# Gated delta rule: the small parts of each head at sixteenths of a head's time, and 11 loads ahead of the overflow loop instead of 14

## The chip, the cores and the metric

The kernel runs on one core of a Trainium2 chip, in one launch. TensorE (PE) multiplies matrices, VectorE (DVE), ScalarE (ACT) and GpSimd (POOL) work on what it leaves in PSUM and on SBUF, and SyncE (SP) issues most of the DMAs. The metric is the device time of the program in microseconds (us), as the median of several runs.

## The reference

A sequence of 512 tokens of width 1024 passes through two blocks. The first has a mixer (a gated delta rule with 8 heads, an HGRN2 recurrence with 8 heads, two gated branches that are merged), cross attention over 256 memory tokens, and a mixture of 32 experts of which each token takes two; the second is two layers of a hybrid of retention, sparse attention and RG-LRU. The change touches the delta rule and the experts.

The delta rule, of one head with chunks of the sequence (q, k, v come from projections, a causal convolution of width 4 and SiLU; q and k are normalised):

```
decay = exp(cum_i - cum_j) for i >= j
A     = strictly lower part of (beta k) k^T * decay
u, w  = (I + A)^-1 [beta v, beta k exp(cum)]
for each chunk:
    v_new = u - w S
    o     = (q exp(cum)) S + (q k^T * decay) v_new
    S     = S exp(last) + (k exp(last - cum))^T v_new
y = rmsnorm(o) * silu(gate)
```

The experts: each token goes to its two best experts of its best group, and `y = (silu(x Wgate) * (x Wup)) Wdown`, weighted and summed over the two. An expert takes 64 tokens at its fixed place; tokens beyond these go through a loop with a run-time number of turns, the overflow loop.

## The kernel before, in words

**The mixer's delta rule (lines 612 to 850, called from `mixer`).** Each head needs four blocks of 128 columns of the projections: q, k, v and the gate g. A block (`Blocks.steps`, lines 275 to 288) is 8 steps over the contraction of 1024; a step is three matmuls of 128 x 128 by 512 columns (`mm3`, lines 218 to 220), since both operands are held as a rounded and a remaining part. In its third step a block also emits the next block's load and its split into two parts (`w_hi` on ACT, line 154, `w_lo` on DVE, line 155).

Beside the blocks run the head's small parts, each a generator that emits a few instructions and yields: `keys` (convolution and SiLU of k, its norm, k k^T, and the way of the matrix A through DRAM into another layout), `queries`, `values`, `gate_out`, `substitute` (36 small operations on DVE, line 743, that invert the 16 x 16 diagonal blocks, then DRAM again), `inverse` (seven steps that build the inverse of I + A from these blocks by matmuls of 64 x 64, the last at line 810, copied by DVE into `Xf` at line 811), and `chunks` (the recurrence over four chunks of 128 tokens, 14 steps). In `chunks` the first step multiplies `Xf` with the values (line 829); every further chunk has a step with the keys and the state (line 824, DVE makes `a_R` of it, line 826), one with `Xf` and `a_R` (line 829, ACT makes `a_vn`), and one that makes the next state (line 836, DVE makes `a_st`, line 841) and the output (lines 843 and 844). At the end `head_out_steps` (lines 421 to 440) normalises and gates the output.

**What sets the order.** `streams` gives every generator a list of times in units of a head: block q from 0 to 0.249, the next head's block k from 0.25, block v from 0.5, block g from 0.75, and the small parts at the numbers of `GDN_AT` (line 612). `weave` sorts all times of all heads, ties by a stream's place in the list, and advances the generators in that order. `Order` ties PE's instructions to the order in which they are emitted. The other engines' order is the planner's: it takes, engine by engine, the ready instruction that was emitted first. So a small part's place decides what PE does between two parts that depend on each other, while DVE, ACT or POOL carry the result over.

PSUM has three banks for the small parts (`ps_c`), three for blocks and two for outputs; most tiles of the small parts in SBUF have two buffers.

**The experts (lines 1497 to 1560 and 1619 to 1715).** Pairs of experts are computed one after the other. Their weights come in loads of 1 MB (12 per pair: gate, up, down, in two parts, for two experts), issued by SP into 16 places. In the list of loads two places are set aside ahead of pair 2 (`OVERFLOW_AT`), where the overflow loop stands; `limit` ends the loads that are issued ahead of the loop at `OVERFLOW_AHEAD` behind them, and `spare` lifts the limit when the loop is emitted. All engines read the number of turns and wait for one another around the loop (line 1652). In this run the loop has no turn.

Of the kernel before, what the change touches and what calls it, by code (L numbers as in the profile page):

```python
# [306 lines left out]
def spread(start, end, n):  # L307

    return [start + (end - start) * k / n for k in range(n)] + [end]


def weave(streams, order):

    parts = sorted((at, k) for k, (_, ats) in enumerate(streams) for at in ats)
    out = [None] * len(streams)
    for _, k in parts:
        try:
            with order:
                next(streams[k][0])
        except StopIteration as s:  # L320
            out[k] = s.value
    return out
# [289 lines left out]
GDN_AT = dict(ones=-0.182, kk=-0.123, kt=0.488, kq=0.687, vt=0.998, fs0=0.248, fs1=0.157, in0=0.628, in1=0.999, ch0=1.02, ch1=2.337)  # L612


class GdnHead:


# [3 lines left out]
    def streams(self, y):  # L621

        block = lambda what, at: (self.block(what), spread(at, at + 0.249, KD))
        P = GDN_AT
        early = 0.0 if self.h else 0.4
        parts = [block("q", 0.0), block("v", 0.5), block("g", 0.75),
                 (self.keys(), [-0.5 - early, P["ones"] - early, P["kk"] - early]), (self.queries(), [0.25, P["kt"], P["kq"]]),
                 (self.values(), [0.75, P["vt"]]), (self.gate_out(), [1.0]), (self.substitute(), spread(P["fs0"] - early, P["fs1"] - early, 4)),
                 (self.inverse(), spread(P["in0"], P["in1"], 6)), (self.chunks(y), spread(P["ch0"], P["ch1"], 13))]
        if self.h:  # L630
            parts.append(block("k", -0.75))
        return [(gen, [self.h + at for at in ats]) for gen, ats in parts]

    def column(self, what):
        return {"q": C_QKV, "k": C_QKV + 1024, "v": C_QKV + 2048, "g": C_OGA}[what] + self.h * 128
# [1 line left out]
    def block(self, what):  # L637
        self.p[what] = yield from self.blocks.steps()
# [517 lines left out]
NE = 32  # L1156
CAP = 64

OVERFLOW_AT, OVERFLOW_AHEAD = 2, 14
FF = 512  # L1160
RINGS = (10, 6)
ORDERED = [mybir.EngineType.PE, mybir.EngineType.DVE, mybir.EngineType.Activation]
# [602 lines left out]
class Layer2:  # L1765
# [33 lines left out]
    def turn(self):  # L1799
        while self.beside:  # L1800
            at, n, gen = min(self.beside, key=lambda x: x[:2])
            if at > self.now:
                return
            self.beside.remove((at, n, gen))
            try:
                self.beside_at(at + next(gen), gen)
            except StopIteration:
                pass
# [820 lines left out]
```

## Time and profile before

| | |
|---|---|
| time, median of 3 runs | 2123.81 us (2123.06 to 2124.79) |
| profiled execution | 2123.9 us, span 2122.1 us, mean granted clock 0.99 |
| PE busy | 2070.5 us of the span, 98% |
| DVE busy | 1122.9 us, 53% |
| ACT busy | 863.6 us, 41% |
| POOL busy | 297.3 us, 14% |
| DMA | 338.92 MB, mean 160 GB/s |

The span runs from the first instruction to the last of one execution; the time of a run is a little longer. A share of busy time is a mean over stages that differ: the delta rule's heads lie between about 325 and 600 us, the experts between about 974 and 1470 us. Matmuls are pipelined and a matmul's end in the profile is modelled, so PE's idle time shows only waits that are longer than the tail of the matmul ahead; shorter ones are seen in the distance between two starts.

### The profile page before, as it was taken

Reading aid. Unit: us, or ns where it says so; the run is one execution under the profiler, and the core shown is the slowest. Engines: PE = TensorE matmul, PEld = TensorE weight load, DVE = VectorE, ACT = ScalarE, POOL = GpSimd, SP = SyncE. Lnnn points to the kernel's source line nnn. Section 1 sums busy time; section 2 is a strip of 40 time slices with the busy share of each in tenths; the row PEclk is TensorE's granted clock in tenths of the full one; section 3 lists DMA queues with packets and bytes.
Section 4 is the critical chain, followed back from the end, with each engine's and each line's share of the span. In section 5 each row is a group of like instructions: output and inputs, shape, how many; then the busy total and the mean of one; then the engine's idle time right before and its main releaser. Section 6 shows DMA issues by size and latency. Waiting matters only on the chain.

```text
span 2122.1 us, 29715 instructions
## 1 busy us (share of the span) xinstructions
PE 2070.5 (98%) x11510; PEld 1475.2 (70%) x11510; DVE 1122.9 (53%) x2375; ACT 863.6 (41%) x1603; POOL 297.3 (14%) x342
## 2 busy tenths in 40 slices
PE   9999999999999999999999999998999999999998
PEld 7888887888777898674444444443777777777776
DVE  3556536888864554435222333224575746475845
ACT  4455534555644344332121111222345644345643
POOL 1122102232321100000000000001022330022330
PEclk9999999999999999999999999999999999999999
DMA  4223333333324344246899999986421215521114
GB/s 152 73 79 80 90 92 84 78 75 73 76 62 126 113 127 126 74 201 245 350 416 425 426 425 425 423 352 228 101 69 31 50 31 169 121 61 41 41 40 139
DMA packets 271651, 338.92 MB, mean 160 GB/s; under 512 B 87594, under 2 KB 229636, under 8 KB 246548
## 3 DMA queue, kind: packets, MB, share of 16 engines
q1 hardware_dynamic: 269636, 332.24, 45.5%
q10 hardware_dynamic: 1296, 2.66, 0.4%
q8 instruction: 92, 1.51, 0.3%
q0 software_dynamic: 576, 2.10, 0.3%
q14 instruction: 51, 0.42, 0.1%
HBM read 329.06 MB, written 7.90 MB: 159 GB/s over the span
## 4 chain that ended last, share of the span: by engine, by line
PE 45%; DVE 4%; ACT 1%; POOL 1%; issue 0%; DVEq 0%; ACTq 0%; POOLq 0%
PE mA L1433 9%; PE mY L1461 5%; PE pd L218 4%; PE pd L219 4%; PE pd L220 4%; PE mC L1413 2%; PE po L2092 2%; PE pc L2069 2%; PE mT L1380 1%; PE mT L1381 1%; PE pc L218 1%; PE pc L220 1%; PE pc L219 1%; PE pc L2047 1%; PE pc L2048 1%; POOL apr L2060 1%
## 5 line engine op out<-in xcount | busy, mean ns | idle before, releaser
L218 PE MATMUL pd<-xhi,w_hi 128*128 128x512 f32 x992 | 420.4, 424 | 1.6 <-DVE ks L1954 1.6
L220 PE MATMUL pd<-xhi,w_lo 128*128 128x512 f32 x992 | 390.7, 394 | 1.0 <-DVE w_lo L155 1.0
L219 PE MATMUL pd<-xlo,w_hi 128*128 128x512 f32 x992 | 388.0, 391 | 0.0
L155 DVE TENSOR_TENSOR w_lo<-w_raw,w_hi 128x1024 fp32r<-128x1024 f32 x199 | 258.2, 1299 | 237.2 <-ACT w_hi L154 231.9
L154 ACT ACTIVATE w_hi<-w_raw 128x1024 fp32r<-128x1024 f32 x204 | 215.2, 1058 | 335.3 <-PE pd L219 228.6
L1433 PE MATMUL mA<-f_w_ring,f_xT 128*64 128x512 f32 x1024 | 232.5, 601 | 0.0
L220 PEld LDWEIGHTS pd<-xhi,w_lo 128*128 128x128 f32 x992 | 186.3, 188 | 42.4 <-DVE w_lo L155 1.4
L218 PEld LDWEIGHTS pd<-xhi,w_hi 128*128 128x128 f32 x992 | 187.5, 189 | 40.1 <-issue 7.2
L219 PEld LDWEIGHTS pd<-xlo,w_hi 128*128 128x128 f32 x992 | 187.5, 189 | 31.9 <-issue 3.4
L1433 PEld LDWEIGHTS mA<-f_w_ring,f_xT 128*64 128x64 f32 x1024 | 72.9, 138 | 137.6 <-issue 135.1
L2060 POOL TENSOR_SCALAR apr<-apr,ars,gl 128x128 f32<-128x128 f32 (+3 forms) x128 | 90.0, 708 | 206.5 <-DVE ars L2056 188.7
L1461 PE MATMUL mY<-f_w_ring,f_aT 128*64 128x512 f32 x512 | 115.0, 595 | 0.0
L1467 DVE SCALAR_TENSOR_TENSOR f_ylo<-mY,f_w,f_yhi 128x512 fp32r<-128x512 f32 x32 | 23.9, 748 | 144.1 <-ACT f_yhi L1466 143.2
L2055 ACT ACTIVATE apr<-pc,anm 128x128 f32<-128x128 f32 (+3 forms) x128 | 66.7, 524 | 68.6 <-DVE anm L2051 67.7
L2397 POOL MEMSET gates<- 128x1024 f32 x1 | 1.0, 957 | 632.8 <-PE mA L1433 632.8
L1461 PEld LDWEIGHTS mY<-f_w_ring,f_aT 128*64 128x64 f32 x512 | 35.4, 137 | 68.4 <-issue 67.0
L2051 DVE TENSOR_REDUCE anm<-pc 128x1 f32<-128x384 f32 (+3 forms) x96 | 57.2, 596 | 40.5 <-PE pc L2049 39.9
L1466 ACT ACTIVATE f_yhi<-mY,f_w 128x512 fp32r<-128x512 f32 x32 | 22.0, 686 | 128.8 <-PE mY L1461 128.8
L1380 PE MATMUL mT<-f_oh,mo_xh 128*128 128x256 f32 x256 | 66.3, 298 | 2.6 <-DVE f_oh L1368 2.0
L1441 ACT ACTIVATE f_a<-f_x 128x512 f32<-128x512 f32 x16 | 10.1, 630 | 132.2 <-DVE f_x L1439 132.2
L1382 ACT ACTIVATE f_xT<-mT,ffn_gain 128x256 f32<-128x256 f32 x64 | 30.3, 474 | 81.5 <-PE mT L1381 75.3
L1381 PE MATMUL mT<-f_oh,mo_xl 128*128 128x256 f32 x256 | 63.5, 287 | 0.0
(633 smaller groups left out, 4047.1 us busy)
## 6 DMA issues: line engine op xcount, KB each, us to landing
f_w_ring<-expert_w_gate SPq DMA_DIRECT2D x64, 1024.0 KB
f_w_ring<-expert_w_up SPq DMA_DIRECT2D x64, 1024.0 KB
f_w_ring<-expert_w_down SPq DMA_DIRECT2D x64, 1024.0 KB
w_raw<-w_in SPq DMA_DIRECT2D x108, 512.0 KB
w_raw<-w_in SPq DMA_DIRECT2D x40, 256.0 KB
w_raw<-w_out SPq DMA_DIRECT2D x16, 512.0 KB
w_raw<-xattn_wkv SPq DMA_DIRECT2D x16, 512.0 KB
w_raw<-w_branch_b SPq DMA_DIRECT2D x8, 512.0 KB
```

What stands on the lines that cost most here:

```text
L154: nc.scalar.activation(hi, src, AF.Copy)
L155: (eng or nc.vector).tensor_tensor(lo, src, hi.bitcast(F32), op=OP.subtract)
L218: nc.tensor.matmul(out, lhs[0], rhs[0], start=start, stop=False)
L219: nc.tensor.matmul(out, lhs[0], rhs[1], start=False, stop=False)
L220: nc.tensor.matmul(out, lhs[1], rhs[0], start=False, stop=stop)
L1380: nc.tensor.matmul(p, xh[:, t, c], oh[:, t, :], start=t == 0, stop=False)
L1381: nc.tensor.matmul(p, xl[:, t, c], oh[:, t, :], start=False, stop=t == NT - 1)
L1433: nc.tensor.matmul(p[j * m:(j + 1) * m], xT[:, k, cols[j]], w_of(mat, j, k, 0), start=k == 0, stop=k == KD - 1)
L1461: nc.tensor.matmul(ps[half][j * m:(j + 1) * m], aT[:, k, j * m:(j + 1) * m], w_of("down", j, k, half), start=k == 0, stop=k == 3)
L2051: nc.vector.tensor_reduce(nm, p, axis=AX.X, op=OP.max, negate=True)
L2055: nc.scalar.activation(pr[:, i, :], p[:, i, :], AF.Exp, bias=nm[:, i:i + 1], accum_out=rs[:, i:i + 1])
L2060: eng.tensor_scalar(pr[:, i, :], pr[:, i, :], rs[:, i:i + 1], self.gl[:, t, c:c + 1], op0=OP.mult, op1=OP.mult)
```

## The change

`streams` splits its list. The blocks and `substitute` keep their times and now stand first in the list; `keys`, `queries`, `values`, `gate_out`, `inverse` and `chunks` get their times rounded to the nearest sixteenth of a head, less 0.001. Parts that fall on one sixteenth are emitted one after the other in the order of the list (a difference in the last digit of two sums can turn it round). In the expert stage `OVERFLOW_AHEAD` is 11 instead of 14.

```diff
+TURNS = 16
...
-        parts = [block("q", 0.0), block("v", 0.5), block("g", 0.75),
-                 (self.keys(), [-0.5 - early, P["ones"] - early, P["kk"] - early]), (self.queries(), [0.25, P["kt"], P["kq"]]),
-                 (self.values(), [0.75, P["vt"]]), (self.gate_out(), [1.0]), (self.substitute(), spread(P["fs0"] - early, P["fs1"] - early, 4)),
+        blocks = [block("q", 0.0), block("v", 0.5), block("g", 0.75), (self.substitute(), spread(P["fs0"] - early, P["fs1"] - early, 4))]
+        if self.h:
+            blocks.append(block("k", -0.75))
+        parts = [(self.keys(), [-0.5 - early, P["ones"] - early, P["kk"] - early]), (self.queries(), [0.25, P["kt"], P["kq"]]),
+                 (self.values(), [0.75, P["vt"]]), (self.gate_out(), [1.0]),
                  (self.inverse(), spread(P["in0"], P["in1"], 6)), (self.chunks(y), spread(P["ch0"], P["ch1"], 13))]
-        if self.h:
-            parts.append(block("k", -0.75))
-        return [(gen, [self.h + at for at in ats]) for gen, ats in parts]
+        turn = lambda at: round(at * TURNS) / TURNS - 0.001
+        return ([(gen, [self.h + at for at in ats]) for gen, ats in blocks] +
+                [(gen, [self.h + turn(at) for at in ats]) for gen, ats in parts])
...
-OVERFLOW_AT, OVERFLOW_AHEAD = 2, 14
+OVERFLOW_AT, OVERFLOW_AHEAD = 2, 11
```

## Rows read from the trace of the kernel before

**Rows 1.** The page, busy time by engine.
```profile
PE 2070.5 (98%) x11510; PEld 1475.2 (70%) x11510; DVE 1122.9 (53%) x2375; ACT 863.6 (41%) x1603; POOL 297.3 (14%) x342
```

**Rows 2.** Stretches: length, busy us of each engine, granted clock, DMA share, GB/s.
```profile
360.00:598.00 238.00, 235.61 (x1789) 190.37 (x1787) 205.47 (x538) 132.72 (x231) 72.55 (x70) 1.00 0.32 76
598.00:601.80 3.80, 0.97 (x6) 0.68 (x6) 3.80 (x29) 2.21 (x5) 0.00 (x0) 1.00 0.01 2
601.80:605.30 3.50, 3.03 (x12) 2.21 (x11) 3.50 (x9) 0.61 (x1) 0.00 (x0) 0.51 0.09 9
```

**Rows 3.** PE's waits, 300 to 660 us: us in total, times, longest.
```profile
PE pc L824 <- DVE a_st L841: 3.0, 6, 0.8
PE pc L829 <- DVE a_R L826: 2.5, 1, 2.5
PE pc L235 <- ACT cs_hi L154: 1.6, 2, 0.8
PE pc L236 <- POOL cs_lo L155: 1.5, 2, 0.9
...
```

**Rows 4.** Order of time on PE from 515.67: start, length, line, operation.
```profile
515.67 0.68 PE L810 MATMUL pc<-a_Xf,a_M 64*64 64x64 f32 x8
516.28 0.50 PE L218 MATMUL pd<-xhi,w_hi 128*128 128x512 f32 x1
...
517.08 0.38 PE L829 MATMUL pc<-a_bv,a_Xf 128*128 128x128 f32 x2
```

**Rows 5.** Order of time on DVE in the same stretch.
```profile
516.39 0.41 DVE L811 COPY a_Xf<-pc 64x256 f32<-64x256 f32 x1
```

**Rows 6.** Order of time on PE, 484.3 to 496.
```profile
486.64 0.39 PE L218 MATMUL pd<-xhi,w_hi 128*128 128x512 f32 x1
...
487.33 0.40 PE L218 MATMUL pd<-xhi,w_hi 128*128 128x512 f32 x1
...
488.49 0.40 PE L220 MATMUL pd<-xhi,w_lo 128*128 128x512 f32 x1
488.86 0.49 PE L829 MATMUL pc<-a_R,a_Xf 128*128 128x128 f32 x2
...
494.22 0.40 PE L220 MATMUL pd<-xhi,w_lo 128*128 128x512 f32 x1
495.06 0.49 PE L824 MATMUL pc<-a_st,a_kT 128*128 128x128 f32 x2 [0.44 <-DVE a_st L841]
```

**Rows 7.** Order of time on DVE, 483 to 495.6.
```profile
484.10 4.45 DVE L743 SCALAR_TENSOR_TENSOR a_tb<-a_blk,a_tb 128x15 f32<-128x15 f32 x24
488.46 0.34 DVE L826 SCALAR_TENSOR_TENSOR a_R<-pc,a_tok,a_bv 128x128 f32<-128x128 f32 x1
488.73 1.65 DVE L743 SCALAR_TENSOR_TENSOR a_tb<-a_blk,a_tb 128x3 f32<-128x3 f32 x12
490.29 0.74 DVE L605 SCALAR_TENSOR_TENSOR cv_a<-pd,vecs,cv_a 128x509 f32<-128x509 f32 x1
...
494.66 0.34 DVE L841 SCALAR_TENSOR_TENSOR a_st<-a_st,a_eclast,pc 128x128 f32<-128x128 f32 x1
```

**Rows 8.** Stretches around the overflow loop.
```profile
1044.00:1048.60 4.60, 4.53 (x19) 2.83 (x17) 3.17 (x6) 0.00 (x0) 0.00 (x0) 1.00 1.00 422
1048.60:1052.40 3.80, 0.00 (x0) 0.00 (x0) 0.90 (x3) 0.00 (x0) 0.00 (x0) 1.00 0.10 37
```

**Rows 9.** Order of time at the loop, all engines.
```profile
1048.13 0.40 PE L1413 MATMUL mC<-f_ylo,f_ohT 128*128 128x512 f32 x1
...
1051.71 0.24 DVE L1639 TENSOR_SCALAR f_sb<-r_slot 128x8 f32<-128x8 f32 x2 [2.46 <-SPq L1652]
...
1053.48 0.80 PE L1391 MATMUL mT<-r_info,f_oh 128*128 128x8 f32 x3 [4.95 <-issue]
```

**Rows 10.** Line 1652, the loop: duration in ns, least, median and most.
```profile
L1652 PEldq COMPARE_BRANCH  x3: 97/193/3601, 1048.0 to 1053.2; - x3
```

**Rows 11.** Order of time on PE, pair 2's down product.
```profile
1074.23 7.04 PE L1461 MATMUL mY<-f_w_ring,f_aT 128*64 128x512 f32 x32
```

## The prediction

> **What bounds the kernel now.** I read the page first, then a table of stretches, PE's waits, and the order of time on PE and DVE in one head. PE is busy 98% of the span [rows 1], so the kernel gains or loses only what PE gains or loses. In the steady part of the gated delta rule PE is busy 235.61 of 238.00 us at a granted clock of 1.00 while DVE works 205.47 us of it [rows 2]: DVE has little spare time, and a small part that waits for DVE is where PE can lose. PE's waits of the whole stage (seven lines, 10.5 us together) are led by L824 and L829, the matmuls of the state chain, both behind DVE [rows 3]. A head takes as much PE work after the change as before: the same blocks, the same matmuls. So the working is about order alone: which small part now stands closer to the one that it needs.
>
> **The new order.** From the diff, a part's place is rounded to the nearest sixteenth of a head, and the four blocks give 32 steps per head, so two block steps stand between neighbouring sixteenths. One step is three matmuls, 487.33 - 486.64 = 0.69 us [rows 6]. Three places change what PE waits for.
>
> **First place: the last inverse step and the first chunk.** Before, `in1` = 0.999 and `ch0` = 1.02 had one block step between them. 0.999 x 16 = 15.98 and 1.02 x 16 = 16.32 both round to 16, and the inverse stands ahead of the chunks in the list: now the chunk's first pair (L829) follows the last inverse matmul (L810) with nothing between. That pair reads `Xf`, which DVE copies (L811) out of L810's PSUM tile. Before, L810 ends at 515.67 + 0.68 = 516.35, the next block step starts at 516.28 [rows 4], and the copy runs from 516.39 to 516.80 [rows 5]. It starts 0.04 us behind L810, so DVE can't be earlier even if idle. From DVE's end to PE's start takes 0.06 us (a_R: 488.46 + 0.34 = 488.80, L829 at 488.86 [rows 6, 7]). L829 can start at 516.86, and PE could have gone on at 516.28: 0.58 us lost. A pair that starts after a wait takes 0.49 us against 0.38 [rows 4, 6]: 0.11 more. 0.69 us for each of 8 heads: **+5.5 us**. No cover exists; a lower bound is 0.58 x 8 = 4.6.
>
> **Second place: the chunk's R behind the substitution.** Before, step 2 of a chunk chain (L824, at 0.223) stood between the third and the last quarter of the next head's substitution (0.203 and 0.225), and DVE follows the order in which the code emits: 24 of the 36 small operations (L743), then a_R, then the last 12 [rows 7]. L829 then started at 488.86, where the matmul ahead of it (488.49, + 0.23 as a third of a step) would have let it start at 488.72 [rows 6]: 0.14 late, 0.25 with the restart. After, L824 moves to 0.249, behind all of the substitution (its end 0.248 isn't rounded), so a_R waits for 12 more operations, 490.29 - 488.73 = 1.56 us [rows 7]: a_R ends at 490.36, PE may start at 490.42. And two steps stand ahead of L829 instead of three: PE is there at 488.72 - 0.69 = 488.03. That makes a wait of 2.4 us, 2.5 with the restart: the upper bound. Two shifts make it smaller: the keys' products, on whose way through DRAM the substitution depends, come one step earlier (four steps of block g ahead of them instead of five: 0.69 us), and PE itself loses 0.69 us at the first place in between. If DVE starts the substitution 1.38 us sooner against PE, the wait is 1.0, with the restart 1.1. The lower bound is no wait, should DVE be ahead of PE by more. I take 1.1, since both shifts follow from the order alone: 1.1 - 0.25 = +0.85 for each of 6 heads, **+5.1 us** (bounds -1.5 and +13.5).
>
> **Third place: the state behind a_st.** L824 at 495.06 came 0.61 us after PE could have had it (494.22 + 0.23 = 494.45 [rows 6]), 0.72 with the restart, since a_st is DVE's turn only at 494.66, behind a convolution that runs from 490.29 on [rows 7]. From L829 at 488.86 to there were 5.59 us, six steps and the small matmuls between; after, the same stands between, in half of the heads without the queries' four transposes (about 0.4 us). From 489.0 PE arrives at 494.2 to 494.6, while DVE's line has moved forward by up to 1.38 us with the substitution: a_st is ready at 495.06 - 1.38 = 493.7. With the late substitution PE arrives 1.4 us later as well, and still doesn't wait. The old wait goes: -0.72 x 6 = **-4.3 us** (bounds 0 and -4.3). What is late next is the first place of the next head.
>
> **The last head** has no k block after it, so its chain stood bare before: PE had 0.97 us of work in 598.0 to 601.8 and then 3.5 us at a clock of 0.51 [rows 2]. After, a_R is later by 1.56 - 1.38 = 0.18 us, and the step that stood ahead of L824 there (Bv7.0 in the code's order) now follows it, 0.69: **+0.9 us** (bounds 0 and 2.2).
>
> The other dependent neighbours keep at least two steps, 1.38 us, against a DVE operation of 0.34 to 0.41 [rows 5, 7] and 0.06 for the handover: 0. Block k, q, v, g and the substitution keep their places; the DMAs of `keys` move with their parts, by a thirty-second of a head at most, and stay between the same weight loads on SP's queue; those of `substitute` stay.
>
> **Eleven loads ahead.** The last of pair 2's twelve 1 MB loads and the first two of pair 3's go out after the empty overflow loop instead of before it. Before, DMA is at 422 GB/s up to 1048.6 and then idles at 37 GB/s until the loop is passed [rows 8]; three loads less, at 2.5 us each, make it idle from about 1041. At the loop PE stands from its last matmul at 1048.13 to 1053.48 [rows 9], of which its branch alone takes 3.60 us [rows 10], in a stretch in which DMA has almost nothing to do: that isn't the loads' doing, so it stays. After the loop five loads stand in the queue instead of two, 5 x 2.5 = 12.4 us from 1052.4, to about 1065. The earliest use of a moved one is in pair 2's down product, which starts at 1074.23 [rows 11]; PE waits for no DMA in this stage, and still won't. 0 us. The bounds: if the engines other than PE, and SP with them, pass as soon as the loads ahead have landed, five loads start beside PE's code load; the nearest row for that is a branch of 3.60 us with DMA idle, and I allow +0.5; a branch that shortens with earlier landings could give back -2.5, DVE's own wait for the loop's release at 1051.71 [rows 9].
>
> The Trainium skill bears on that bound: DMA: Bandwidth & Descriptors, "Queues, rings and completion order", says that a DMA engine takes its queues in turn, a packet at a time. By this rule a code load beside five weight loads waits for a packet and not for all of them, so the sum would stay at 0; no row before shows the two together, since DMA is idle during the branch [rows 8].
>
> **Sum**: 5.5 + 5.1 - 4.3 + 0.9 + 0 = +7.2 us. The profiled execution took 2123.9 us for a span of 2122.1 (1.8 around it), 0.1 over the median of 2123.81, so the time is 2123.9 + 7.2 = 2131.1, rounded 2131.
>
> **Rivals.** Changes within 0.2%, 4.2 us, can't be told from none here.
>
> - *Hidden by DVE.* DVE reaches the substitution early enough that a_R is never late: 5.5 - 1.5 - 4.3 = -0.3, time 2123.6. For it: a_R itself takes 0.34 us, and in the page's slices DVE isn't full everywhere. Against: DVE is busy 86% of this stretch [rows 2], and it kept to the emitted order [rows 7].
> - *a_R fully late.* The substitution starts where it did: 5.5 + 13.5 - 4.3 + 2.2 = +16.9, time 2140.8. For it: from the fifth head on, the rounded places fall in an order in which the queries' convolution is also emitted ahead of a_R (0.74 us an operation [rows 7]).
> - *The clock falls in every head.* In the last head, after 3.8 us with 0.97 us of matmuls, the clock went to 0.51 for 3.5 us [rows 2], 1.75 us lost. If the new waits do that in six heads: +10.5 on top, 2141.6. Against: one wait of 0.6 us per head left the clock at 1.00 throughout 360 to 598 [rows 2], and the new waits lie some 10 us apart. The Trainium skill, TensorE: Matmul & The Clock Gate, "What's actually happening", says that the array's clock is released by activity and throttled again after idleness; the last head's drop agrees (0.51), and the rule speaks against any change that adds waits, without saying that waits of 1 us are enough.
> - *Faster.* The other side: gaps that were three steps and are now four (steps 0 to 1 and 3 to 4 of a chunk chain; the fifth to the sixth inverse step, from one to two) give DVE room, and all of the stage's waits of 10.5 us [rows 3] and the last head's slow clock (1.75) go, with only the first place to pay: 5.5 - 10.5 - 1.75 = -6.8, time 2117. It decides if DVE's line stays ahead of PE in every head, the first and the last too. Against: the waits on L235 and L236, 3.1 us together [rows 3], have no wider gap in the new order.
> - *The loop passes sooner.* PE's branch ends with the landing of the loads ahead: -2.5 on the forecast, 2128.6.
>
> **Chances**: forecast 0.50 (its own range 2127 to 2137), hidden 0.19, a_R fully late 0.10, clock 0.05, faster 0.11, loop 0.05. The range of 2120 to 2142 leaves out about 0.15. Slower by over 0.2% (above 2128.1): 0.45 of the forecast, the late and the clock cases and a part of the loop's, 0.64; within 0.2%: 0.24; faster: 0.12.
>
> **What would show it.** Right: a new wait of about 0.5 us on L829 behind DVE's L811 in each of eight heads; L826 behind all 36 L743 and a wait on L829 behind it; L824's waits of 0.6 gone; the loop's pause near 5 us as before, with DMA idle from about 1041. Wrong: L829 without wait after L811 (the first place, and with it the sign); L826 still between the operations of L743 (the second); dips of the clock between 360 and 600; a pause at the loop of under 4 us.

## The result and the profile after

The changed kernel takes 2149.2 us (2148.9 to 2150.4, four runs) against 2123.4 for the kernel before in the same runs: a ratio of 1.0119, 95% interval 1.0107 to 1.0131, 25.8 us slower. The direction was forecast, the size was not: 2149 lies above the range of 2120 to 2142.

The changed kernel's lines are 4 to 6 higher: L829 is now L835 (the chunk's matmul with `Xf`), L824 is L830 (with the state), L826 is L832 (`a_R`), L743 is L749 (the substitution), L811 is L817, L836 is L842, L839 and L841 are L845 and L847 (`a_st`), L1391 is L1397.

PE does the same number of instructions as before [rows 1]; its share of the span fell by a point.

```profile
PE 2078.9 (97%) x11510; PEld 1484.2 (69%) x11510; DVE 1124.1 (52%) x2375; ACT 866.3 (40%) x1603; POOL 300.6 (14%) x342
```

The loss lies in the delta rule: from the first to the last matmul with `Xf` 280 us pass before the change (370.5 to 650.6) and 307 behind it (370.4 to 677.6), 27 us more, where the whole span grew by 25.6. A head's period, from one drop of the clock to the next (460.8 to 501.8 below), is 41.0 us; it was 37.1 (L829 at 479.98 and 517.08). Stretches of the changed kernel, columns as in rows 2: one head, the 3.8 us ahead of its drop, and the drop.

```profile
460.80:501.80 41.00, 37.43 (x277) 30.79 (x275) 32.56 (x86) 21.32 (x37) 10.81 (x11) 0.96 0.29 69
...
498.00:501.80 3.80, 0.74 (x4) 0.26 (x3) 3.80 (x24) 1.27 (x3) 0.00 (x0) 1.00 0.02 2
...
501.80:505.20 3.40, 3.40 (x9) 2.82 (x10) 3.40 (x5) 1.51 (x3) 1.39 (x1) 0.50 0.10 13
```

PE's waits between 300 and 690 us, which answer to rows 3:

```profile
PE pc L835 <- DVE a_R L832: 19.8, 7, 4.4
PE pc L835 <- DVE a_Xf L817: 4.1, 8, 0.5
...
PE pc L830 <- DVE a_st L847: 0.3, 1, 0.3
```

So `a_Xf` is late in eight heads, as forecast; `a_st` no longer is, as forecast; but `a_R` is late by 19.8 us in seven places instead of 2.5 in one, where 1.1 us per head was forecast, and the clock falls in six heads instead of one. The seven waits are 1.41, 2.38, 2.40, 3.06, 3.03, 3.06 and 4.42 us long, and each from the second on is followed by a stretch at a granted clock of 0.50 or 0.51. PE and DVE in the head of the rows above, in order of time:

```profile
489.72 0.49 PE L835 MATMUL pc<-a_bv,a_Xf 128*128 128x128 f32 x2 [0.51 <-DVE a_Xf L817]
...
493.27 0.39 PE L842 MATMUL pc<-a_vn,a_kt 128*128 128x128 f32 x2
...
496.92 0.38 PE L830 MATMUL pc<-a_st,a_kT 128*128 128x128 f32 x2
...
498.30 0.40 PE L220 MATMUL pd<-xhi,w_lo 128*128 128x512 f32 x1
501.75 0.80 PE L835 MATMUL pc<-a_R,a_Xf 128*128 128x128 f32 x2 [3.06 <-DVE a_R L832]
```

```profile
493.01 0.69 DVE L428 COPY ho_o<-po 128x512 f32<-128x512 f32 x1 [0.32 <-ACT ho_sq L426]
493.69 0.29 DVE L845 COPY a_st<-pc 128x128 f32<-128x128 f32 x1
493.90 0.79 DVE L745 TENSOR_TENSOR a_blk<-a_blk,a_bt 128x256 f32<-128x256 f32 x1
494.73 6.06 DVE L749 SCALAR_TENSOR_TENSOR a_tb<-a_blk,a_tb 128x15 f32<-128x15 f32 x36
500.71 0.73 DVE L605 SCALAR_TENSOR_TENSOR cv_a<-pd,vecs,cv_a 128x509 f32<-128x509 f32 x1
501.37 0.33 DVE L832 SCALAR_TENSOR_TENSOR a_R<-pc,a_tok,a_bv 128x128 f32<-128x128 f32 x1
```

At the overflow loop PE restarts after a pause of 4.6 us (4.95 before [rows 9]), and DMA falls idle at least 5 us sooner against it than before: PE's last matmul ahead of the loop starts at 1074.75 and ends at 1075.15, and DMA moves next to nothing from 1070.0 on.

```profile
1079.78 0.38 PE L1397 MATMUL mT<-r_info,f_oh 128*128 128x8 f32 x1 [4.63 <-issue]
```

```profile
1070.00:1074.80 4.80, 4.80 (x22) 3.33 (x20) 3.31 (x5) 0.00 (x0) 0.00 (x0) 1.00 0.00 2
```

### The profile page after: what moved, and what is told of

It is laid out like the page before. It is cut to its first block, busy times and chain, and to the rows that moved or that the text cites. A ratio compares the mean times of both kernels' runs of the same rounds, so it can differ in the third digit from the quotient of the medians.

```text
span 2147.7 us, 29733 instructions
## 1 busy us (share of the span) xinstructions
PE 2078.9 (97%) x11510; PEld 1484.2 (69%) x11510; DVE 1124.1 (52%) x2375; ACT 866.3 (40%) x1603; POOL 300.6 (14%) x342
```

## The experiments

Costs in us below are the ratio to the kernel before, in the same runs, times 2123.4; brackets hold the 95% interval.

### The parts of the change alone

**The eleven loads alone**, in the kernel before:

```diff
-OVERFLOW_AT, OVERFLOW_AHEAD = 2, 14
+OVERFLOW_AT, OVERFLOW_AHEAD = 2, 11
```

> The kernel before with 11 loads ahead of the overflow loop, and nothing else. If the loads are no part of the loss: 2123.4 us, within 1 us of before, a pause of PE at the loop near 5 us and a stretch with idle DMA some 7 us longer. Rival: the three loads that go out later cost PE something behind the loop: 2124 to 2128 us, with a wait of PE on a DMA that the kernel before does not have. Rival on the other side: the branch ends earlier with the landings: 2121 us.

2122.4 us, ratio 0.9995 [0.9986, 1.0005]; PE's pause at the loop 5.2 us. The loads show no part in the loss.

**The first place alone**, in the kernel before (the position of step 0 in the list of times):

```diff
-... (self.chunks(y), spread(P["ch0"], P["ch1"], 13))]
+... (self.chunks(y), [0.9991 if n == 0 else at for n, at in enumerate(spread(P["ch0"], P["ch1"], 13))])]
```

> The kernel before, in which only step 0 of each chunk chain is moved directly behind the last inverse step. If the places add up: eight waits of 0.5 us and nothing else, +5.5, 2128.6 us. If DVE's line binds: the changed place also delays what DVE does behind the copy by up to 0.7 us in each head (ACT takes another operation ahead of the square that DVE's copy of the output follows), so the waits on a_R and a_st grow by as much, 4 us more: 2133 us. If DVE makes up for it: 2123 to 2125 us.

2129.0 us, ratio 1.0024 [1.0014, 1.0034], +5.1 [3.0, 7.2]: the forecast's own +5.5. The waits on `a_Xf` are 4.1 us in 8 places, those on `a_R` and `a_st` as before. The second theory missed here: nothing grows behind the copy.

**The second place alone**, the same edit with `1.249 if n == 2`:

> The kernel before, in which only step 2 of each chunk chain is moved to 0.249 of the next head, behind the whole substitution; three block steps still stand between it and step 3. By the order of the kernel before, a_R ends 1.56 us later, at 490.36 in the head of the prediction, and PE could start at 488.72: a wait of 1.7 us where 0.14 were, with the restart 1.56 more in 6 heads, +9.4, less the 0.72 that PE then no longer waits for a_st, -4.3: 2128.5 us. If a wait of 1.7 us also drops the clock in each head, 1.7 us more for each of 6: 2139 us. If DVE has spare time that the order of the kernel before does not show: 2123 to 2125 us.

2130.3 us, ratio 1.0029 [1.0015, 1.0043], +6.2 [3.2, 9.1]. PE's waits:

```profile
PE pc L829 <- DVE a_R L826: 13.5, 7, 3.8
```

Five of the seven are 1.45 to 1.70 us long, one 1.85, the last 3.75; no wait on `a_st` is left, and in the heads the clock stays up until the last one. The two places alone make some 11 us together, and the change made 25.8.

### One place undone in the changed kernel

These five differ in the set of steps that keep their old times:

```diff
-[(gen, [self.h + turn(at) for at in ats]) for gen, ats in parts])
+[(gen, [self.h + turn(at) for at in ats]) for gen, ats in parts[:-1]] +
+[(parts[-1][0], [self.h + (at if n in (2,) else turn(at)) for n, at in enumerate(parts[-1][1])])])
```

**Step 2 undone**, `(2,)`:

> The changed kernel, in which only step 2 of each chunk chain (the matmul with keys and state, and DVE's a_R) keeps its old place, ahead of the last quarter of the substitution. If the second place makes both the long waits on a_R and, by them, the drops of the clock: both go, the first place stays (8 waits of 0.5 us behind a_Xf), and the time is 2123.4 + 5.5 - 2.7 (the waits on a_st that the change removed) = 2126 us, between 2123 and 2129. Rival: the first place takes part in the drops of the clock, so some of them stay: 2132 to 2140 us.

2145.1 us, ratio 1.0102 [1.0085, 1.0119]: only 4 of the 25.8 us come back, where 23 were expected. The waits on `a_R` fell from 19.8 to 6.2 us, but now `a_st` is late, 9.5 us in 7 places instead of 0.3 in one. Ahead of the last head one drop of the clock is left, behind a wait of 1.81 us on `a_st`; another such wait, as long, is followed by none.

**Step 0 undone**, `(0,)`:

> The changed kernel, in which only step 0 of each chunk chain keeps its old place, one block step behind the last inverse step. If DVE's line moves with PE's (it waits for PE shortly before), the 8 waits of 0.5 us behind a_Xf go and the waits on a_R stay as long as they are: 2149.2 - 8 x 0.69 = 2143.7 us. Rival: the substitution starts at its own time, whatever PE does, so what PE saves at the first place it waits at the second: 2148 to 2149 us, with waits on a_R of about 3.1 us in the heads that have 2.4 now.

2145.2 us, ratio 1.0103 [1.0086, 1.0120]: the waits on `a_Xf` go, those on `a_R` stay, near the first theory's 2143.7. PE saved a step ahead of the substitution and waits as long behind it:

```profile
PE pc L835 <- DVE a_R L832: 19.7, 7, 4.4
```

The four executions differ: 2137.8 us the profiled one, 2144.7 to 2146.2 the others.

**Both undone**, `(0, 2)`:

> The changed kernel, in which steps 0 and 2 of each chunk chain keep their old places; all else is rounded. If the places add up, as in the prediction, a_Xf, a_R and a_st are all in time: 2119 to 2121 us. If DVE's line from the copy of a_Xf to the second state is what binds (it was 15.7 us before, 17.4 with step 2 alone undone), then DVE comes 0.7 us sooner than there, a_R is in time, and the waits on a_st stay at 1.4 us in 6 or 7 heads, against 0.6 before: 2128 us, between 2125 and 2131.

2139.4 us, ratio 1.0082 [1.0060, 1.0104], above both. The first line is the one that counts:

```profile
PE pc L830 <- DVE a_st L847: 12.9, 7, 2.8
PE pc L835 <- DVE a_R L832: 6.1, 7, 2.1
```

`a_R` is 0.7 us late since two block steps, not three, stand between steps 2 and 3; and `a_st` is 1.8 to 2.2 us late, since in DVE's order `ylo` and another operation (L373) now stand ahead of it:

```profile
500.23 1.20 DVE L155 TENSOR_TENSOR w_lo<-w_raw,w_hi 128x1024 fp32r<-128x1024 f32 x1
501.36 0.67 DVE L155 TENSOR_TENSOR ylo<-ho_o,yhi 128x512 fp32r<-128x512 f32 x1
502.33 0.43 DVE L373 TENSOR_SCALAR cv_L<-cv_L 128x512 f32<-128x512 f32 x1 [0.30 <-ACT cv_L L372]
502.68 0.34 DVE L847 SCALAR_TENSOR_TENSOR a_st<-a_st,a_eclast,pc 128x128 f32<-128x128 f32 x1
```

**Step 13 undone as well**, `(0, 2, 13)`. It is the last part of a head's output and has no matmul in it, so PE's order is that of the run before, instruction by instruction; only DVE's and ACT's differ.

> The changed kernel with steps 0, 2 and 13 of each chunk chain at their old places: beside the run with steps 0 and 2 alone, only the last part of a head's output moves, which has no matmul in it, so PE's order is the same in both. If DVE's order behind the substitution is what binds (in that run ylo and another DVE operation stood ahead of a_st, and DVE took 12.3 us from the substitution's start to the end of a_st against 10.9 before), DVE takes about 10.9 again, the waits on a_st fall from 1.8 us to 0.4 or 0.6 in 7 heads, and the time is 2139.4 - 9 = 2130 us, between 2127 and 2133. Rival: what counts is PE's order, the same here: 2138 to 2140 us.

2129.0 us, ratio 1.0023 [1.0014, 1.0033]: 10 us less with the same order on PE. `a_st` is ahead of the two operations again, and its waits fall from 12.9 to 6.3 us:

```profile
PE pc L830 <- DVE a_st L847: 6.3, 7, 2.8
```

```profile
496.07 0.68 DVE L439 TENSOR_TENSOR ho_o<-ho_o,g_s 128x512 f32<-128x512 f32 x1
496.67 0.34 DVE L847 SCALAR_TENSOR_TENSOR a_st<-a_st,a_eclast,pc 128x128 f32<-128x128 f32 x1
...
498.08 0.69 DVE L155 TENSOR_TENSOR ylo<-ho_o,yhi 128x512 fp32r<-128x512 f32 x1
```

**All 14 steps undone**, `range(14)`:

> The changed kernel, in which all 14 steps of the chunk chains keep their old places; keys, queries, values, gate and inverse are rounded as in the change. If the loss lies in the order of the chunk chains' steps against the substitution and the convolutions on DVE: the waits of before come back (a_R in time, a_st 0.6 late in 6 heads), 2123.4 us, between 2121 and 2126. Rival: the rounding of the other parts (the keys' products, the inverse) carries a part of the loss: 2128 us or more.

2132.5 us, ratio 1.0035 [1.0021, 1.0049], +7.4 [4.5, 10.4]: the waits of the chains are those of before, but others come, with the rival's 2128 or more: 4.4 us in 7 places on L236 behind GpSimd's `cs_lo` (1.5 in 2 before [rows 3]) and 2.8 on the inverse's L776. So the rounding of the keys and of the inverse can cost time of its own. But in the changed kernel these waits don't stand (L236 has 1.5 us in 2 places, as before), so how much of the 25.8 us is theirs is not shown.

**The ties.** From the fourth of the seven waits on, in the fifth head's time, a convolution (L605) stands ahead of `a_R`; in the first three it stands behind it. The sums rounded to four digits:

```diff
-[(gen, [self.h + turn(at) for at in ats]) for gen, ats in parts])
+[(gen, [round(self.h + turn(at), 4) for at in ats]) for gen, ats in parts])
```

> The changed kernel with the sums rounded to four digits, so that parts on one sixteenth follow the list in every head: the second chunk's a_R is then emitted ahead of the next head's convolution in all heads, not only in the first four. If the 3.06 us against 2.4 in the later heads are this convolution (0.66 us from its start to a_R's): the waits on a_R fall to 2.4 us in all of them, 4 x 0.66 = 2.6 us less: 2146.5 us, the drops of the clock as they are. If the shorter wait is short enough to keep the clock up: 2140 us. Rival: another operation takes the convolution's place: 2149 us.

2145.0 us, ratio 1.0096 [1.0079, 1.0113], 1.5 us below the 2146.5 expected. The waits on `a_R` fall from 19.8 to 17.2 us, the 2.6 expected; the drops stay.

**Thirty-seconds** (`TURNS = 32`):

> The changed kernel with thirty-seconds instead of sixteenths (one number changed). The first chunk step then stands one block step behind the last inverse step, step 2 ahead of the substitution's last quarter and four block steps ahead of step 3, and the last output part falls behind step 3 as before. By DVE's line: no wait on a_Xf or a_R, a_st 0.6 late as before or in time, 2121 to 2125 us. Rival: rounding of any kind costs (the order of the inverse's and the keys' parts): 2130 us or more.

2138.4 us, ratio 1.0069 [1.0052, 1.0085]. A miss, and the rival's 2130 or more: `a_Xf` is in time and `a_st` nearly so (0.9 us in 2 places), but `a_R` is late by 9.0 us in 9 places and L236 behind `cs_lo` by 8.2 in 7. A finer grid makes other close neighbours.

### Wait and clock apart

**PE kept busy ahead of the late `a_R`:**

```diff
-            p = ps_c.tile([128, 128], F32, name="pc")
+            whole = ps_c.tile([128, S], F32, name="pc")
+            p = whole[:, 0:128]
+            for _ in range((5, 9, 9, 12, 12, 12, 16, 0)[h] if c == 1 else 0):
+                x = self.blocks.x
+                nc.tensor.matmul(whole, x[:, 0, 0:128], x[:, 0, :], start=True, stop=True)
             nc.tensor.matmul(p, Xf[:, c, :], R, start=True, stop=True)
...
+            blocks.x = xhi
```

> The changed kernel with extra matmuls of a block's shape (0.23 us each, their result is overwritten) in front of the second chunk's matmul that waits for a_R: 5, 9, 9, 12, 12, 12 and 16 of them in the seven heads whose waits were 1.4, 2.4, 2.4, 3.1, 3.0, 3.1 and 4.4 us. The time at which a_R is ready does not change; only PE is not idle until then. If the idle PE drops the clock, the drops of the changed kernel between 419 and 591 us (20.6 us at half the clock) go, and the time is 2149.2 - 10 = 2139 us; if the last head's drop goes too, 2137. Rival: the clock falls for another reason, or the drops hide behind waits: 2148 to 2151 us.

2137.6 us, ratio 1.0061 [1.0044, 1.0077], 11.7 us less than the changed kernel; the expectation was 10 to 12. No drop is left in the delta rule from 360 us on (from 620 to 640 us the granted clock is 1.00 as well):

```profile
360.00:620.00 260.00, 252.32 (x1850) 205.40 (x1849) 214.17 (x567) 137.31 (x234) 73.70 (x70) 1.00 0.29 69
```

Of these 11.7 us about 1.7 are the last head's drop (3.4 us at half the clock), which the kernel before has as well [rows 2]. So of the 25.8 us some 10 are the clock, and the rest, 15 or 16, are waits. The split is good to a few us: the interval of this run is 3.5 us to either side, and in its profile a drop near 322 us, which the changed kernel's profile has and which lies ahead of all added matmuls, is missing too.

### What holds the substitution

**The keys' product two block steps later**, and the way through DRAM with it:

```diff
-GDN_AT = dict(ones=-0.182, kk=-0.123, ...
+GDN_AT = dict(ones=-0.182, kk=-0.0625, ...
```

> The changed kernel with the product of the keys (and so the way of the matrix through DRAM) one sixteenth, two block steps, later: 1.4 us. If DVE's queue sets the substitution's start (the copies ahead of it end 2.7 us after the DMAs), nothing moves: 2149 us, waits on a_R of 2.4 and 3.1 us as in the changed kernel. If the way through DRAM sets it, as the prediction's second place has it, each wait on a_R grows by up to 1.4 us: 7 x 1.4 = 9.7 us more, 2159 us, or by a part of that.

2148.9 us, ratio 1.0125 [1.0108, 1.0142], as the changed kernel. Only the first of the seven waits on `a_R` grew (1.41 to 3.11 us); the others are 2.3 to 3.0 and 4.4 us. Behind the first head the way through DRAM binds nothing.

**Two copies from DVE to ACT**, PE's order unchanged:

```diff
-    nc.vector.tensor_copy(o, p_o)
+    nc.vector.tensor_copy(o, p_o) if extra is None else nc.scalar.activation(o, p_o, AF.Copy)
...
-                    nc.vector.tensor_copy(sn, p)
+                    nc.scalar.activation(sn, p, AF.Copy)
```

> The changed kernel with two copies out of PSUM on ACT instead of DVE: a head's output (ho_o, 0.69 us) and the first state (a_st, 0.29 us). PE's order is the same, and so is DVE's for all else. If DVE's queue sets the substitution's start, it starts 1.6 us sooner (behind a_eclast, at the equivalent of 493.1 instead of 494.7), the waits on a_R fall from 2.4 and 3.1 us to 0.8 and 1.4, 11 us in all, and the clock stays up: 2149.2 - 11 - 10 = 2128 us, between 2125 and 2134. If the clock falls all the same: 2138. Rival: the way through DRAM sets it, and it starts as late as before: 2147 to 2149 us.

2145.2 us, ratio 1.0102 [1.0085, 1.0119]: the start came as expected, the time did not. The substitution starts 3.42 us behind the chunk's first matmul (490.43 against 487.01) instead of 5.01, 1.6 sooner; but it takes 7.06 us instead of 6.06, and the waits only fall to 1.8 and 2.5 us, with the clock down behind five of the seven. Its first operation takes as long as GpSimd's operation beside it. DVE and GpSimd, in order of time:

```profile
489.97 0.43 DVE L745 TENSOR_TENSOR a_blk<-a_blk,a_bt 128x256 f32<-128x256 f32 x1
490.43 1.27 DVE L749 SCALAR_TENSOR_TENSOR a_tb<-a_blk,a_tb 128x15 f32<-128x15 f32 x1
```

```profile
490.39 1.28 POOL L430 TENSOR_TENSOR ho_sq<-ho_sq,a_qsq 128x512 f32<-128x512 f32 x1 [5.06 <-ACT ho_sq L426]
492.42 1.30 POOL L155 TENSOR_TENSOR cs_lo<-ho_sq,cs_hi 128x512 fp32r<-128x512 f32 x1 [0.74 <-ACT cs_hi L154]
```

**Without these two GpSimd operations**, first in the changed kernel, then with the copies on ACT too:

```diff
-        nc.gpsimd.tensor_tensor(sq, sq, extra, op=OP.add)
-    sq = exact_parts(e, pool, sq)
+        hi = pool.tile([128, S], F32R, name="cs_hi", bufs=1); nc.scalar.activation(hi, sq, AF.Copy)
+    sq = exact_parts(e, pool, sq) if extra is None else (hi, hi)
```

> The changed kernel without the two GpSimd operations of a head's output: the addition of q's squares and the remainder of the squares are left out (the output is no longer the reference's); PE's and DVE's order is the same. If GpSimd's operation holds one operation of the substitution (1.3 us instead of 0.24) and slows the product ahead of it (0.79 instead of 0.41), the waits on a_R shrink by 1.4 us to 1.0 and 1.6 us: 10 us less, 2139 us, and if waits of 1.6 us leave the clock up, as they did in the kernel before with step 2 alone moved, 10 more: 2129 us. Rival: the long operation has another cause: 2149 us.

> The same two GpSimd operations left out, and the two copies on ACT: the substitution starts 3.4 us behind the first chunk's matmul and takes 4.9 us, so a_R is ready 9.4 us behind that matmul, where PE needs it at 8.8: waits of 0.6 us in the later heads and none in the others, the clock up. 2149.2 - 16 - 10 = 2123 us, between 2121 and 2128. Rival: the two effects overlap, and it gives no more than the first alone.

2131.9 us, ratio 1.0035 [1.0023, 1.0046], near the 2129 expected, and 2125.1 us, ratio 1.0006 [0.9996, 1.0016], where 2121 to 2128 was: 24 of the 25.8 us come back with PE's order as it is in the change. In both the substitution takes 4.98 us. Waits of 0.96 to 1.61 us are left in the first, of 0.47 to 0.92 in the second (the last head's 2.96 and 2.31 apart), and the clock stays up ahead of the last head in both. PE's waits on `a_R` in the changed kernel without the two operations:

```profile
PE pc L835 <- DVE a_R L832: 11.1, 7, 3.0
```

And with the copies on ACT as well:

```profile
PE pc L835 <- DVE a_R L832: 5.2, 6, 2.3
```

**Less work for DVE in the kernel before**: a head's product with the gate and `ylo` on GpSimd.

```diff
-    nc.vector.tensor_tensor(o, o, gate, op=OP.mult)
-    split(e, o, y[0], y[1])
+    (nc.vector if extra is None else nc.gpsimd).tensor_tensor(o, o, gate, op=OP.mult)
+    split(e, o, y[0], y[1], None if extra is None else nc.gpsimd)
```

> The kernel before, in which two operations of each head's output in the delta rule (the product with the gate, 0.60 us on DVE, and the remaining part ylo, 0.61) run on GpSimd. PE's order is the same. If DVE's line from the copy of a_Xf to a_st binds PE, the product's 0.60 us leave it ahead of a_st and the six waits of 0.6 us with their restarts of 0.11 go: 2123.4 - 4.3 = 2119 us. If GpSimd's own operations slow DVE's down by as much (a product of 0.41 us took 0.79 beside one on GpSimd): 2123 us. If the last head's output becomes late: 2125 us or more.

2124.1 us, ratio 0.9995 [0.9986, 1.0005]. All six waits on `a_st` are gone, as in the first theory, but the time is the same instead of 4.3 us less: a head still takes 37.0 us, where it took 37.1 with 36.7 of work for PE. New waits on the inverse's L770, 1.0 us in 5 places, make up a part. No version here is clearly faster than the kernel before.

## Why the prediction was wrong

**First place: right.** Eight waits of 0.5 us, and +5.1 [3.0, 7.2] alone against +5.5.

**Second place: this step failed.** It took a wait of 2.4 us as the upper bound and then subtracted 1.38, because the keys' products come one step earlier and PE itself loses a step at the first place; both were to bring the substitution forward against PE. Neither does: the term of +5.1 us came out as 15.3 us of waits (1.41 to 3.06 in six heads). The substitution doesn't wait for the DRAM path: in the kernel before DMA had been silent for 1.65 us when it started, in the changed kernel it was silent up to 492.5, and what it moved from there to the start at 493.9 were two loads issued at 492.52 and 492.96. Stretches of the kernel before and of the changed one (the last but one column is DMA's share):

```profile
482.00:483.65 1.65, 1.65 (x11) 1.41 (x10) 1.65 (x5) 0.86 (x2) 1.23 (x1) 1.00 0.00 0
```

```profile
491.20:492.50 1.30, 1.30 (x9) 1.16 (x8) 0.69 (x1) 1.15 (x3) 0.00 (x0) 1.00 0.00 0
```

It stands in DVE's queue behind the copy of the first state, and that copy waits for PE's own step 1. Two rows of the kernel before show it, on PE and on DVE:

```profile
482.72 0.38 PE L836 MATMUL pc<-a_vn,a_kt 128*128 128x128 f32 x2
```

```profile
483.14 0.29 DVE L839 COPY a_st<-pc 128x128 f32<-128x128 f32 x1
```

The copy starts 0.04 us behind the end of the matmul (482.72 + 0.38 = 483.10), and so it does in every head of both kernels. DVE hardly idles ahead of it: the copy of the head's output ends at 483.18, so that one holds the substitution almost as late.

```profile
482.50 0.68 DVE L428 COPY ho_o<-po 128x512 f32<-128x512 f32 x1
```

So DVE starts afresh in each head from PE's step 1, and whatever PE lost or the keys gained ahead of it cancels. From that matmul on the sum closes. Before, PE needed 488.72 - 482.72 = 6.00 us from step 1 to step 3 and `a_R` was 0.14 late. After, PE needs 498.53 - 493.27 = 5.26 us (one block step fewer), 0.74 less; DVE has the 12 operations more, 1.56, and from the fourth wait on the convolution, 0.66; 0.14 is left over: 3.1 us more, and `a_R` is 501.75 - 498.53 = 3.22 late. Without the convolution, in the second and third wait, it is 2.4 us, the prediction's own upper bound; with it 3.1, above that bound, which left out the convolution that one of the rivals named. Runs show each half of it: with PE's step at the first place given back the waits stayed, later keys changed them in the first head alone, and with the two copies on ACT the substitution came forward by the 1.6 us that this cause gives.

**Third place: right in the row, wrong in the reason.** The waits on `a_st` went (3.0 to 0.3 us), but because PE now comes late. Where step 2 has its old place and `a_R` is made earlier they return, longer than before: 9.5 and 12.9 us. The prediction moved DVE's line as a whole and left its order as it was; but the last part of a head's output, rounded too, comes one block step earlier, and `ylo` and L373 pass ahead of `a_st`. The run with step 13 undone shows that on an unchanged PE.

**The last head** was forecast at +0.9, bounds 0 and 2.2: its wait went from 2.5 to 4.4 us, with the drop of the clock as before, so 1.9.

**Eleven loads: right**, 0 with a pause at the loop of 5.2 us alone and 4.6 in the change.

**The rivals.** "a_R fully late" (2140.8) and "the clock falls in every head" (2141.6) were priced one by one, with chances of 0.10 and 0.05, and the second was argued away by waits of 1 us that were themselves the misjudged step. So the sum had no term for the clock, which the run with PE kept busy puts at some 10 us. They are not alternatives: a fully late `a_R` is the longer wait that drops the clock. Together they give 2123.9 + 16.9 + 10.5 = 2151.3, against 2149.2. The drops shown agree with the Trainium skill, TensorE: Matmul & The Clock Gate, "What's actually happening", as the prediction cited it: the clock is taken back after idleness.

What stays open: the waits by their rows, 17.3 more on `a_R`, 4.1 on `a_Xf` and 2.7 less on `a_st`, are 18.7 us, and the run with PE kept busy leaves 15 or 16. The difference of some 3 us lies within the interval of that run. But the kernel before did not get faster either when its 3.0 us of waits on `a_st` went. Whether PE makes up some of its waiting elsewhere in the heads is not shown.

## What to carry to other kernels

Before a wait is shortened because "everything ahead of it moves too", find the operation in the waiting engine's queue that ties it to PE, and count from there: what lies ahead of that tie cancels. Places in a list that orders only one engine by hand also reorder the queues of all others, so a small part without a matmul can cost as much as one with a matmul. When two rivals are cause and effect, price them together.

## What the runs showed of the hardware

**GpSimd holds DVE up for a whole operation.** In the run with the copies on ACT, one operation of the substitution, 128 x 15 elements, took 1.27 us beside a GpSimd product of 1.28 us, where none of the 36 takes over 0.23 when both GpSimd operations are left out. In the changed kernel the longest of the 36 took 1.30 beside `cs_lo`, with a median of 0.21:

```profile
L749 DVE SCALAR_TENSOR_TENSOR a_tb<-a_blk,a_tb x36: 202/212/1303, 494.7 to 500.6; 128x3 f32<-128x3 f32 x4, 128x2 f32<-128x2 f32 x4, 128x1 f32<-128x1 f32 x4, 128x7 f32<-128x7 f32 x3
```

With both GpSimd operations left out the 36 took 4.98 us instead of 6.06. The Trainium skill, SBUF — State Buffer, "Who interferes with whom", says that DVE and GpSimd share a port pair under an exclusive lock, and that a DVE instruction with two SBUF inputs contends with a GpSimd instruction that reads SBUF. The runs agree: one instruction waits for the whole of the other, and the rest take as long as without it. The kernel before has this too (its longest of the 36 took 1.27 us), so it is no part of what the change added; the change made PE wait for it. GpSimd's share of 14% in the page doesn't tell where that falls; here it fell into the one stretch in which PE waited for DVE.

**Short waits were enough to lower the clock.** In the changed kernel each of the six waits on `a_R` of 2.38 us and more was followed by 3.4 to 6.9 us at the lower of the two levels (1.2 GHz, granted clock 0.50 or 0.51). With the second place alone, six waits of 1.45 to 1.85 us were followed by none. In between it varies: of two waits of 1.83 and 1.85 us in the run with the copies on ACT the second was followed by a drop, and the first wait of the run with later keys, 3.11 us, by none.
